# A scheduler that knows VectorE's change of rows, and a newly chosen order of two layers' front pieces

## The chip, the cores and the metric

One core of a Trainium2 chip runs the whole program. The metric is device time in microseconds (us) of one execution, median of the runs.

## The reference

Two encoder layers over 512 tokens of width 1024, float32. In each layer one projection of the normalised input feeds two branches and two gates; the branches are merged, then a feed-forward part (MLP) follows.

```python
h = rms_norm(x, norm1_g[l]) * (1.0 + sc1) + sh1
proj = h @ w_in[l]
y_a = diff_attention(...)            # 4 heads: softmax(q1 k1) - lam * softmax(q2 k2), times v
y_b = gated_deltanet(...)            # 4 heads, both directions, chunks of 64, a triangular solve
merged = g_a * (y_a @ w_branch_a[l]) + g_b * (y_b @ w_branch_b[l])
x = x + gt1 * (merged @ w_out[l])
h = rms_norm(x, norm2_g[l]) * (1.0 + sc2) + sh2
x = x + gt2 * (jnp.square(jax.nn.relu(h @ w_mlp1[l])) @ w_mlp2[l])
```

## The kernel before

The kernel first records all its operations (class `Plan`, `add` at L195) and only then orders them. `schedule` (L250) walks through a model of the engines: each has a time at which it is free, each operation a cost (`cost`, L438) and a delay after what it depends on (`LAG`), and the engine that is free first takes the ready operation with the lowest key. The key is a level (0 for the chains, then evictions, weights, dense products, side work) and, within a level, the place in which the code recorded it. `HOLD` (L424) keeps an engine from starting lower work just before higher work comes in. The resulting order is issued as it stands, so on the chip every engine, and the DMA queue on SyncE (SP), runs its own list strictly in that order and waits on semaphores.

Dense products are split in three: weights are cast to a high part by ScalarE (`whi`), VectorE forms the rest (`wlo`), and TensorE adds three products with the input's parts `hh` and `hl`. So each block of dense weights needs one VectorE subtraction of 128x1024, named `wlo_` and the block, before TensorE can go through it. 24 products of 512 columns make one such block of the gates (`d_g`) or of z (`d_z`); 96 of 256 columns make a pair of blocks of the attention's projections (`d_da`).

The front of a layer is everything up to the branch products. It consists of 28 pieces, recorded in the sequence that `ORDER` (L477) gives for each layer:

- `d`h, `z`h: projections of delta-net head h with their convolutions, and its gate z.
- `a`h (`gdn_a`, L959): norms, the products of keys with keys (`kk`) and the decay, from which the triangular matrices L come; these go through DRAM (`scrL`) into a packed tile `XA`, 32 partitions a head.
- `b0`, `b2` (`gdn_b`, L1032): the triangular inverse of two heads at once, in place in `XA`: a chain of 30 pairs of VectorE operations and a memset, each waiting for the one before. `b0` (heads 0 and 1) works on partitions 0 to 63, `b2` (heads 2 and 3) on 64 to 127.
- `c`h (`gdn_c`, L1047): `XA` goes back through DRAM (`scrT`) into tiles `DT` and `X`; first the products `pn` and `px`, then the state's recurrence over four steps (`pv`, `pS`), the outputs `pog`, and their transposes `ogT`.
- `q`j, `k`j, `v`j: the attention's projections for two heads each; q and k are normalised, rotated, transposed and written to DRAM.
- `t`h (`attention`, L1162): loads q2, k2 and vt of head h, then four blocks of scores `sc`, two maxima and exponentials each, the difference `pr`, transposes `aTp` and products `po`.

```python
for j in range(1, NB - 1):                                   # gdn_b; X is XA's 64 rows of two heads
    dve.tensor_tensor(out=tv, in0=X[:, j+1:NB, j:j+1]..., in1=X[:, j:j+1, 0:j]..., op=ALU.mult)
    op = dve.tensor_tensor(out=X[:, j+1:NB, 0:j], in0=X[:, j+1:NB, 0:j], in1=tv, op=ALU.add)
```

After the pieces come eight blocks of gate products and eight more in turn with the branch products `d_brb` (which need all four `c`), then `d_bra` (which need all four `t`). Gate products, at the dense level, fill TensorE wherever the pieces leave it free. What the code records from the first `d_bra` of a layer to the next front does not depend on the pieces' sequence.

In this text layer one and layer two are l = 0 and l = 1.

Of the kernel before, what the change touches and what calls it, by code (L numbers as in the profile page):

```python
# [23 lines left out]
H = 4  # L24
# [135 lines left out]
class Op:  # L160
    __slots__ = ("eng", "fn", "args", "kw", "key", "preds", "succs", "tiles", "cost", "n", "est", "start", "end",
                 "seq", "ins", "done", "left", "shared", "tried")


class Eng:
    def __init__(self, plan, *names):
# [14 lines left out]
class Plan:  # L181
# [68 lines left out]
    def schedule(self):  # L250
        names = ("pe", "act", "dve", "pool", "sp")
        free_at = {e: 0.0 for e in names}
        ready = {e: [] for e in names}
        future = {e: [] for e in names}
        free = {c: [(0.0, i) for i in range(n)] for c, n in self.slots.items()}
        live = {}
        blocked = {}
        dma_free, flying, shared = 0.0, [], 0.0
        busy, fast = [0.0], [False]
        order = []  # L260
        ops = self.ops
        for op in ops:
            op.left = len(op.preds)
            for q in op.preds.values():
                q.succs.append(op)

        def need(op):
            return [t for t in op.tiles if t.slot is None]

        def offer(op):  # L270

            ts = need(op)
            for t in ts:
                if t.cls not in free:
                    continue
                c, g = free[t.cls], t.grp
                want = sum(u.cls == t.cls for u in ts)
                if len(c) < want + t.keep or live.get(g, 0) >= self.limits.get(g, 1 << 30):
                    return (t.cls, g)
            for t in ts:  # L280
                if t.cls not in free:
                    t.slot = -1
                    continue
                c = free[t.cls]
                best = min(range(len(c)), key=lambda i: c[i])
                t.since, t.slot = c.pop(best)
                live[t.grp] = live.get(t.grp, 0) + 1
            est = max(t.since for t in op.tiles) if op.tiles else 0.0
            for e in op.eng:
                at = max([est] + [q.end + lag(q.eng[0], e) for q in op.preds.values()])  # L290
                heapq.heappush(future[e], (at, op.key, op))
            return None

        def push(op):
            why = offer(op)
            if why:
                heapq.heappush(blocked.setdefault(why, []), (op.key, op))

        def retry(cls):
            for why in [w for w in blocked if w[0] == cls]:  # L300
                while blocked[why]:
                    op = blocked[why][0][1]
                    new = offer(op)
                    if new == why:
                        break
                    heapq.heappop(blocked[why])
                    if new:
                        heapq.heappush(blocked.setdefault(new, []), (op.key, op))

        for op in ops:  # L310
            if not op.left:
                push(op)
        todo = len(ops)
        while todo:
            best = None
            for e in names:
                f, r = future[e], ready[e]
                while f and (f[0][2].done or f[0][0] <= free_at[e]):
                    _, k, op = heapq.heappop(f)
                    if not op.done:  # L320
                        heapq.heappush(r, (k, op))
                while r and r[0][1].done:
                    heapq.heappop(r)
                if r:
                    s = free_at[e]
                elif f:
                    s = f[0][0]
                else:
                    continue
                if best is None or s < best[0]:  # L330
                    best = (s, e)
            if best is None:
                raise RuntimeError("no operation can go on: " + self.held(blocked, order))
            s, e = best
            f, r = future[e], ready[e]
            if not r:
                free_at[e] = s
                while f and f[0][0] <= s:
                    _, k, op = heapq.heappop(f)
                    if not op.done:  # L340
                        heapq.heappush(r, (k, op))
            op = heapq.heappop(r)[1]
            if e != "sp" and op.key[0] >= 0 and HOLD[int(op.key[0])] is not None:

                most, slack = HOLD[int(op.key[0])]
                end = s + op.cost[op.eng.index(e)]
                soon = [x[0] for x in f if x[1][0] < most and x[0] < end - slack and not x[2].done]
                if soon:
                    heapq.heappush(f, (min(soon) + 0.001, op.key, op))
                    continue  # L350

            wait = max([0.0] + [at + lag(o, e) for t in op.tiles if t.cls == "B" for o, at in t.use.items() if o != e])
            if op.shared and e in ("dve", "pool") and shared > s:
                if e == "pool" and wait <= shared:

                    s = wait = shared
                wait = max(wait, shared)
            if wait > s:
                heapq.heappush(f, (wait, op.key, op))
                continue  # L360
            c = op.cost[op.eng.index(e)]
            if e == "pe":

                while s >= (len(busy)) * CLOCK_WINDOW:
                    fast.append(busy[-1] > CLOCK_BUSY * CLOCK_WINDOW)
                    busy.append(0.0)
                busy[-1] += c if op.kw.get("rhs") is None or op.kw["rhs"].shape[-1] > 1 else 0.0
                c *= 1 if fast[-1] else 2
            if any(max(s, free_at[o]) + d < s + c for o, d in zip(op.eng, op.cost) if o != e and o not in op.tried):

                op.tried.add(e)
                continue
            op.done = True
            if op.shared and e in ("dve", "pool"):
                shared = s + c
            op.eng = (e,)
            op.start = s
            if e == "sp":
                dma_free = max(dma_free, op.start + DMA_LEAD) + c
                op.end = dma_free + DMA_TAIL  # L380
                flying.append(op.end)
                free_at[e] = max(op.start + DMA_STEP, flying[-DMA_DEPTH] if len(flying) >= DMA_DEPTH else 0.0)
            else:
                op.end = op.start + c
                free_at[e] = op.end
            order.append(op)
            todo -= 1
            for t in op.tiles:
                t.use[e] = op.end
                t.end = max(t.end, op.end)  # L390
                t.left -= 1
                if not t.left and t.cls in free:
                    free[t.cls].append((t.end + 130.0, t.slot))
                    live[t.grp] -= 1
                    retry(t.cls)
            for q in op.succs:
                q.left -= 1
                if not q.left:
                    push(q)
        return order  # L400
# [21 lines left out]


HOLD = ((0, 600.0),) * 4 + ((3, 100.0),)  # L424
DMA_LEAD, DMA_TAIL, DMA_STEP, DMA_DEPTH = 1100.0, 2400.0, 475.0, 8
CLOCK_WINDOW, CLOCK_BUSY = 3413.0, 0.4
LAG = {"pe": {"pe": 0, "act": 197, "dve": 197, "pool": 197, "sp": 100},
# [10 lines left out]
def cost(eng, fn, dst, ins, kw):  # L438
# [21 lines left out]
    if fn == "memset":  # L460
# [13 lines left out]
GS, NYF, KEEPM = (3, 5), 2, (3, 2)  # L474


ORDER = ("d0 a0 d1 a1 z1 q0 z0 b0 c0 z2 c1 d2 d3 a3 z3 k0 a2 b2 k1 c2 q1 v0 v1 t0 t1 t2 t3 c3",  # L477
         "k1 d0 d1 q0 d2 z1 a0 z0 k0 a1 b0 c0 z2 a2 d3 c1 a3 b2 q1 v0 t0 z3 v1 t1 t2 c2 c3 t3")


@with_exitstack
def encoder(ctx, tc, a, out):
# [3 lines left out]
    pe, act, dve, pool, sp = (Eng(pl, e) for e in ("pe", "act", "dve", "pool", "sp"))  # L486
# [273 lines left out]
    for l in range(DEPTH):  # L760
# [286 lines left out]
        def gdn_c(h, XA):  # L1047
# [24 lines left out]
            for d in range(2):  # L1072
                NTr = Y([P, NT, P], "NT")
                if d == 0:
                    c1, full, ks = slice(0, P - NB), slice(0, P), slice(0, P)
                else:
                    c1, full, ks = slice(NB, P), slice(0, P - NB), slice(0, P - NB)
# [3 lines left out]
                for n in range(1, 4):  # L1081
                    m = P - NB * n
                    rows, cs = (slice(0, m), slice(NB * n, P)) if d == 0 else (slice(0 if n == 1 else P - m, P), slice(0, m))
                    ps, op = four("px", NTr[ks, :, rows], X[ks, d, :, cs], rows, cs)
# [43 lines left out]
            for t in (0, 3, 1, 2):  # L1128
                mms = []
                for d in range(2):  # L1130
                    s = t if d == 0 else NT - 1 - t
# [16 lines left out]
            dve.scalar_tensor_tensor(out=y, in0=pT, scalar=col(O_OUTG + l, 1), in1=ztile[h], op0=ALU.mult, op1=ALU.mult)  # L1148
            yh, yl = Y([P, S], "ybh", F32R), Y([P, S], "ybl", F32R)
            split(yh, yl, y)  # L1150
            ybh.append(yh)
            ybl.append(yl)

        gate = {}

        def opt(*names):
            return [gate[n] for n in names if n in gate]

        ybh, ybl, yah, yal = [], [], [], []


        def attention(h):  # L1162
# [57 lines left out]
            y, yh, yl = Y([P, S], "ya"), Y([P, S], "yah", F32R), Y([P, S], "yal", F32R)  # L1220
            act.activation(y, pT, AF.Copy, scale=subg)
            split(yh, yl, y)
            yah.append(yh)
            yal.append(yl)


        mrg, sga = {}, {}
# [10 lines left out]
        for piece in ORDER[l].split():  # L1238
            kind, h = piece[0], int(piece[1])
# [306 lines left out]
```

## Time and profile before

| | |
|---|---|
| median of 3 runs | 1641.72 us (1641.08 to 1642.95) |
| the profiled execution | 1642.87 us, of which 1641.1 us from first to last instruction |
| TensorE busy | 1597.4 us (97%) |
| VectorE busy | 1349.3 us (82%) |
| ScalarE busy | 834.5 us (51%) |
| GpSimd busy | 162.7 us (10%) |
| mean granted TensorE clock | 0.995 |

The two fronts run from about 45 to 424 us and from 828 to 1234 us of the span; the rest is branch output products and MLP. A busy TensorE is not one at its peak: records of matmuls overlap, so that a stretch can be counted busy although its matmuls start further apart than elsewhere. What a stretch lost is therefore read by counting its matmuls and multiplying by the pace at which they follow each other where nothing is waited for.

### The profile page before, as it was taken

Reading aid. Unit: us, or ns where it says so; the run is one execution under the profiler, and the core shown is the slowest. Engines: PE = TensorE matmul, PEld = TensorE weight load, DVE = VectorE, ACT = ScalarE, POOL = GpSimd, SP = SyncE. Lnnn points to the kernel's source line nnn. Section 1 sums busy time; section 2 is a strip of 40 time slices with the busy share of each in tenths; the row PEclk is TensorE's granted clock in tenths of the full one; section 3 lists DMA queues with packets and bytes.
Section 4 is the critical chain, followed back from the end, with each engine's and each line's share of the span. In section 5 each row is a group of like instructions: output and inputs, shape, how many; then the busy total and the mean of one; then the engine's idle time right before and its main releaser. Section 6 shows DMA issues by size and latency. Waiting matters only on the chain.

```text
span 1641.1 us, 25365 instructions
## 1 busy us (share of the span) xinstructions
PE 1597.4 (97%) x9136; PEld 1379.0 (84%) x9136; DVE 1349.3 (82%) x2995; ACT 834.5 (51%) x1596; POOL 162.7 (10%) x170
## 2 busy tenths in 40 slices
PE   6999999999999999999989999989999999999998
PEld 4788898888899888888888889868888988888887
DVE  7989798799899999985988987998627885767676
ACT  4563352575366645454557435555423674636361
POOL 0232040001300000000023112200003000000000
PEclk9999999999999999999999999999999999999999
DMA  9242625545677585745333331714243625252542
GB/s 378 113 120 67 198 86 169 184 123 184 246 268 272 199 314 178 296 148 211 118 110 104 123 103 65 174 39 123 77 150 121 215 81 197 86 200 83 204 155 78
DMA packets 107728, 260.78 MB, mean 159 GB/s; under 512 B 27841, under 2 KB 40769, under 8 KB 107602
## 3 DMA queue, kind: packets, MB, share of 16 engines
q1 hardware_dynamic: 107602, 259.16, 45.9%
q8 instruction: 72, 1.18, 0.3%
q14 instruction: 54, 0.44, 0.1%
HBM read 242.31 MB, written 16.81 MB: 158 GB/s over the span
## 4 chain that ended last, share of the span: by engine, by line
PE 82%; DVE 12%; DMA 2%; ACT 2%; issue 1%; SPq 1%; POOL 0%; DVEq 0%; ACTq 0%; POOLq 0%
PE d_m L420 18%; PE m2x L420 11%; PE d_g L420 9%; PE d_out L420 6%; PE m2y L420 5%; PE d_da L420 4%; PE d_dn L420 4%; PE d_m1f L420 3%; PE d_brb L420 3%; PE m2z L420 3%; PE d_bra L420 3%; PE px L420 2%; PE d_z L420 2%; PE pv L420 2%; PE pog L420 1%; PE sc L420 1%
## 5 line engine op out<-in xcount | busy, mean ns | idle before, releaser
L420 PE MATMUL d_m<-hh,whi_m 128*128 128x512 f32 x448 | 174.3, 389 | 0.0
L420 PE MATMUL d_m<-hl,whi_m 128*128 128x512 f32 x448 | 174.3, 389 | 0.0
L420 PE MATMUL d_m<-hh,wlo_m 128*128 128x512 f32 x448 | 174.3, 389 | 0.0
L420 DVE TENSOR_TENSOR m2lo<-m,m2hi 128x1024 fp32r<-128x1024 f32 x112 | 132.2, 1217 | 9.1 <-ACT m2hi L420 8.3
L420 ACT CAST m2hi<-m 128x1024 fp32r<-128x1024 f32 x112 | 114.0, 1048 | 48.5 <-DMA m<-in_w_m_dram 23.3
L420 DVE SCALAR_TENSOR_TENSOR ada<-ada,cb 128x1024 f32<-128x1024 f32 x96 | 116.3, 1222 | 3.5 <-DMA ada<-in_ada_w_dram 3.5
L420 PE MATMUL d_da<-whi_da,hl 128*128 128x256 f32 x384 | 110.0, 288 | 0.0
L420 PE MATMUL d_da<-whi_da,hh 128*128 128x256 f32 x384 | 109.5, 287 | 0.0
L420 PE MATMUL d_da<-wlo_da,hh 128*128 128x256 f32 x384 | 108.0, 288 | 0.1
L420 ACT ACTIVATE relu<-d_m 128x512 f32<-128x512 f32 x56 | 33.5, 599 | 145.0 <-PE d_m L420 144.9
L420 PE MATMUL d_g<-hh,whi_g 128*128 128x512 f32 x256 | 102.4, 400 | 0.0
L420 PE MATMUL d_g<-hh,wlo_g 128*128 128x512 f32 x256 | 102.3, 399 | 0.0
L420 PE MATMUL d_g<-hl,whi_g 128*128 128x512 f32 x256 | 101.8, 398 | 0.0
L420 PEld LDWEIGHTS d_m<-hh,wlo_m 128*128 128x128 f32 x448 | 84.1, 188 | 17.5
L420 PEld LDWEIGHTS d_m<-hh,whi_m 128*128 128x128 f32 x448 | 84.1, 188 | 17.5
L420 PEld LDWEIGHTS d_m<-hl,whi_m 128*128 128x128 f32 x448 | 84.1, 188 | 17.3
L420 ACT CAST whi_m<-raw_m 128x1024 fp32r<-128x1024 f32 x56 | 58.8, 1050 | 48.5 <-DMA raw_m<-in_w_mlp_dram 42.6
L420 PE MATMUL d_dn<-hh,wlo_dn 128*128 128x512 f32 (+1 forms) x208 | 79.3, 382 | 0.9 <-DVE wlo_dn L420 0.9
L420 PE MATMUL d_dn<-hl,whi_dn 128*128 128x512 f32 (+1 forms) x208 | 79.2, 381 | 0.0
L420 PE MATMUL d_dn<-hh,whi_dn 128*128 128x512 f32 (+1 forms) x208 | 77.5, 380 | 0.0
L420 DVE TENSOR_TENSOR m<-m,m 128x1024 f32<-128x1024 f32 x64 | 77.5, 1217 | 0.0
L420 DVE TENSOR_TENSOR wlo_m<-raw_m,whi_m 128x1024 fp32r<-128x1024 f32 x56 | 67.9, 1221 | 10.5 <-ACT whi_m L420 10.2
(325 smaller groups left out, 4749.3 us busy)
## 6 DMA issues: line engine op xcount, KB each, us to landing
m<-in_w_m_dram SPq DMA_DIRECT2D x112, 512.0 KB, 4.5
ada<-in_ada_w_dram SPq DMA_DIRECT2D x96, 512.0 KB, 6.1
raw_m<-in_w_mlp_dram SPq DMA_DIRECT2D x56, 512.0 KB, 4.6
raw_g<-in_w_g_dram SPq DMA_DIRECT2D x32, 512.0 KB, 4.5
raw_out<-in_w_out_dram SPq DMA_DIRECT2D x32, 512.0 KB, 4.2
raw_dn<-in_w_dn_dram SPq DMA_DIRECT2D x24, 512.0 KB, 6.0
raw_da<-in_w_da_dram SPq DMA_DIRECT2D x24, 512.0 KB, 4.9
xs<-xT SPq DMA_DIRECT2D x24, 256.0 KB, 2.6
```

The costliest lines, as they stand in the source:

```text
L420: op.ins = getattr(eng[op.eng[0]], fn)(*[real(v) for v in op.args], **{k: real(v) for k, v in op.kw.items()})
```

## The change

In the scheduler's model a VectorE operation whose output lies on other partitions (first and last one compared) than that of the operation before it now starts at least `OTHER_ROWS` = 110 ns after the end of that one. `ORDER` holds a new sequence for both layers. The lists of head outputs (`ybh`, `ybl`, `yah`, `yal`) are filled by head number, since heads no longer come in order. No operation is added or removed but for which engine takes a copy that two engines may take: VectorE gets 11 copies `aT` in place of 6.

```diff
 class Op:
+    def rows(self):
+        return self.kw.get("out", self.args[0] if self.args else None).region()[:2]
...
             c = op.cost[op.eng.index(e)]
+            if e == "dve":
+                rows = op.rows()
+                if rows != dve_rows:
+                    s = max(s, dve_end + OTHER_ROWS)
...
                 free_at[e] = op.end
+                if e == "dve":
+                    dve_rows, dve_end = rows, op.end
...
+OTHER_ROWS = 110.0
...
-ORDER = ("d0 a0 d1 a1 z1 q0 z0 b0 c0 z2 c1 d2 d3 a3 z3 k0 a2 b2 k1 c2 q1 v0 v1 t0 t1 t2 t3 c3",
-         "k1 d0 d1 q0 d2 z1 a0 z0 k0 a1 b0 c0 z2 a2 d3 c1 a3 b2 q1 v0 t0 z3 v1 t1 t2 c2 c3 t3")
+ORDER = ("d0 a0 d1 a1 z1 z0 q0 b0 z2 c0 c1 d3 d2 a3 k0 a2 b2 c2 z3 q1 k1 v1 v0 t0 t2 t3 c3 t1",
+         "d0 k1 d1 q0 d2 z1 a0 z0 d3 k0 z2 a1 b0 c0 a2 v0 t0 c1 a3 b2 q1 c2 z3 v1 c3 t3 t1 t2")
...
-            ybh.append(yh)
-            ybl.append(yl)
+            ybh[h] = yh
+            ybl[h] = yl
...
-        ybh, ybl, yah, yal = [], [], [], []
+        ybh, ybl, yah, yal = ([None] * H for i in range(4))
```

VectorE, layer two, inside `b2` (rows 64x... are its chain, `64x13x18` being 13 rows of 18 elements; 128-row entries belong to the attention heads t0 and t1: maxima `mxv`, sums `cc`, `rc`, the difference `pr`). Before:

```order
2091 L420 TENSOR_TENSOR yal<-ya,yah 128x512
2092 L420 TENSOR_TENSOR XA<-XA,btmp 64x13x18
2093 L420 COPY r_11990<-rc 128x1
2094 L420 TENSOR_TENSOR cc<-sums,rc 128x1
2095 L420 TENSOR_TENSOR btmp<-XA 64x228
2096 L420 TENSOR_TENSOR cc<-cc,nlams 128x1
2097 L420 SCALAR_TENSOR_TENSOR nb<-mxv,qsc 128x1
2098 L420 TENSOR_TENSOR XA<-XA,btmp 64x12x19
2099 L420 SCALAR_TENSOR_TENSOR pr<-pr,cc 128x512
2100 L420 TENSOR_TENSOR btmp<-XA 64x220
```

Now:

```order
2010 L431 TENSOR_TENSOR btmp<-XA 64x168
2011 L431 TENSOR_TENSOR XA<-XA,btmp 64x24x7
2012 L431 TENSOR_TENSOR btmp<-XA 64x184
2013 L431 TENSOR_TENSOR XA<-XA,btmp 64x23x8
2014 L431 TENSOR_TENSOR btmp<-XA 64x198
2015 L431 TENSOR_TENSOR XA<-XA,btmp 64x22x9
2016 L431 TENSOR_TENSOR wlo_g_11987<-raw_g_11849,whi_g_11984 128x1024
2017 L431 TENSOR_TENSOR btmp<-XA 64x210
```

101 instructions of the two attention heads and of others stood between the chain's; six stand there now (one `yal`, five `wlo`), so that VectorE changes between rows that start at 0 and rows that start at 64 22 times in the layer, where it was 126 times (layer one: 18 and 22).

TensorE, layer two, where c2's first products `pn` stand. Before (attention heads t1 and t2 between them):

```order
5150 L420 MATMUL d_g_12509<-hh_8884,whi_g_11996 128x512
5151 L420 MATMUL po<-vt,aT 128x128 x4
5152 L420 MATMUL pn<-DT,L 128x96 x2
5153 L420 MATMUL aTp<-cst,pr 128x128 x4
5154 L420 MATMUL pn<-DT,L 128x96 x2
```

Now (gate blocks alone ahead of them and between them):

```order
5158 L431 MATMUL d_g_12225<-hh_8931,whi_g_12115 128x512
5159 L431 MATMUL d_g_12225<-hl_8940,whi_g_12115 128x512
5160 L431 MATMUL d_g_12225<-hh_8931,wlo_g_12123 128x512
5161 L431 MATMUL pn<-DT,L 128x96
5162 L431 MATMUL d_g_12225<-hh_8937,whi_g_12115 128x512
5163 L431 MATMUL d_g_12225<-hl_8946,whi_g_12115 128x512
5164 L431 MATMUL pn<-DT,L 128x96 x3
```

Between the key products `kk` of a3 and this first `pn`, TensorE's list before held 217 matmuls of 512 columns (`d_g`, `d_z`, `sc`), 138 of 256 (`d_da`), 52 float32 products of 128 columns and 60 transposes; now it holds 236, 33, 26 and 20. The heads t1, t2, t3 stand behind c3 now, where d_brb and the last gate blocks are; t0 stands ahead of a3's `kk`.

The DMA queue, layer two, where t0's loads stand (`vt_...<-vst` writes v of two heads to DRAM). Before:

```order
406 L420 DMA vt_11413<-vst 128x2x256
407 L420 DMA scrL_11425<-LT 32x4x32 x4
408 L420 DMA raw_g_11499<-in_w_g_dram 128x1024
409 L420 DMA raw_g_11519<-in_w_g_dram 128x1024
410 L420 DMA q_11523<-qT_9954 64x2x512 x2
411 L420 DMA k_11536<-kT_9280 64x2x512 x2
412 L420 DMA XA<-scrL_11425 32x1024
413 L420 DMA vt<-vt_11413 128x4x128
```

Now:

```order
397 L431 DMA kT_9757<-qkst 128x2x256
398 L431 DMA vt_10861<-vst 128x2x256 x2
399 L431 DMA raw_g_10876<-in_w_g_dram 128x1024
400 L431 DMA q_10925<-qT_9954 64x2x512 x2
401 L431 DMA k_10944<-kT_9757 64x2x512 x2
402 L431 DMA vt<-vt_10861 128x4x128
403 L431 DMA raw_g_10966<-in_w_g_dram 128x1024
404 L431 DMA gb<-grow_9370 128x512 x2
```

They were issued among a2's transfers and come now right behind c0's first ones, ahead of a2's and a3's `gb`, with 69 `d_da` products and 76 small products of c0 and c1 on TensorE between v0's last product and t0's first `sc`.

## Rows read from the trace of the kernel before

**Rows 1.** Page, part 1 (busy us, share of span, instructions) and part 4

```profile
PE 1597.4 (97%) x9136; PEld 1379.0 (84%) x9136; DVE 1349.3 (82%) x2995; ACT 834.5 (51%) x1596; POOL 162.7 (10%) x170
...
## 4 chain that ended last, share of the span: by engine, by line
PE 82%; DVE 12%; DMA 2%; ACT 2%; issue 1%; SPq 1%; POOL 0%; DVEq 0%; ACTq 0%; POOLq 0%
```

**Rows 2.** Engines' busy time by stretch: b2 of layer one, b2 of layer two

```profile
core 0: us, PE busy (x) PEld busy (x) DVE busy (x) ACT busy (x) POOL busy (x), PEclk, DMA share, GB/s
...
252.14:278.90 26.76, 26.76 (x119) 22.15 (x118) 24.62 (x64) 6.77 (x9) 2.33 (x6) 1.00 0.33 118
...
1051.56:1109.42 57.86, 48.67 (x253) 37.21 (x251) 54.03 (x162) 31.51 (x71) 4.51 (x8) 1.00 0.26 64
```

**Rows 3.** Groups of VectorE instructions in b2 of layer one: count, busy, mean ns

```profile
L420 DVE TENSOR_TENSOR XA<-XA,btmp 64x30 f32<-64x30 f32 (+14 forms) x30 | 9.9, 329 | 1.0
...
L420 DVE TENSOR_TENSOR wlo_g<-raw_g,whi_g 128x1024 fp32r<-128x1024 f32 x4 | 4.9, 1225 | 0.1
```

**Rows 4.** The same in b2 of layer two

```profile
L420 DVE TENSOR_TENSOR XA<-XA,btmp 64x30 f32<-64x30 f32 (+14 forms) x30 | 9.9, 330 | 0.9
```

**Rows 5.** VectorE's timeline (start, duration) in b2 of layer two

```profile
1086.02 0.40 DVE L420 TENSOR_TENSOR XA<-XA,btmp 64x234 f32<-64x234 f32 x1
1086.45 0.15 DVE L420 COPY r<-rc 128x1 f32<-128x1 f32 x1
1086.52 0.15 DVE L420 TENSOR_TENSOR cc<-sums,rc 128x1 f32<-128x1 f32 x1
```

**Rows 6.** VectorE's timeline in b0 of layer one

```profile
120.89 0.33 DVE L420 TENSOR_TENSOR btmp<-XA 64x184 f32<-64x184 f32 x1
121.15 0.73 DVE L420 SCALAR_TENSOR_TENSOR cacc<-d_dn,cols,cacc 128x510 f32<-128x510 f32 x1
121.81 0.33 DVE L420 TENSOR_TENSOR XA<-XA,btmp 64x184 f32<-64x184 f32 x1
```

**Rows 7.** Waits of TensorE in b2 of layer two: total us, times, longest

```profile
PE aTp L420 <- DVE pr L420: 5.3, 6, 1.5
```

**Rows 8.** The chain that ended last, by time: start, us, matmuls following each other

```profile
658.85 43.52 PE d_m L420 x192
...
232.76 15.23 PE d_da L420 x127
...
1006.50 2.01 PE pog L420 x18
```

**Rows 9.** Timelines: last kk products ahead of b2, b2's first instructions, layer two, layer one

```profile
1019.58 1.06 PE L420 MATMUL kk<-kqv 128*128 128x128 f32 x8
...
1051.56 0.20 DVE L420 TENSOR_TENSOR btmp<-XA 64x30 f32<-64x30 f32 x1
...
215.53 0.72 PE L420 MATMUL kk<-kqv 128*128 128x128 f32 x5
...
252.14 0.21 DVE L420 TENSOR_TENSOR btmp<-XA 64x30 f32<-64x30 f32 x1 [2.69 <-DMA XA<-scrL]
252.38 0.21 DVE L420 TENSOR_TENSOR XA<-XA,btmp 64x30 f32<-64x30 f32 x1
```

**Rows 10.** Engines by stretch: from b2's memset to c2's first pn, layer two

```profile
1109.42:1118.60 9.18, 8.65 (x51) 7.31 (x52) 9.08 (x27) 6.36 (x14) 0.10 (x1) 1.00 0.41 106
```

**Rows 11.** Engines by stretch: from c2's first pn to d_bra, layer one and two

```profile
287.39:424.13 136.74, 136.73 (x852) 118.08 (x853) 122.44 (x352) 79.38 (x193) 8.34 (x6) 1.00 0.56 183
...
1118.60:1234.09 115.49, 115.49 (x694) 99.90 (x693) 62.42 (x165) 46.61 (x111) 4.54 (x4) 1.00 0.36 118
```

**Rows 12.** Layer one, b0's memset to c0's first pn: engines, and TensorE's timeline

```profile
162.91:173.52 10.61, 8.02 (x28) 5.90 (x29) 8.68 (x30) 1.89 (x3) 2.94 (x2) 0.84 0.73 209
...
164.21 0.56 PE L420 MATMUL d_z<-hh,wlo_z 128*128 128x512 f32 x1 [3.50 <-DVE wlo_z L420]
```

**Rows 13.** Layer two, t0's loads: DMA queue's timeline, then the chain that ended last

```profile
1028.39 0.38 SPq L420 DMA_DIRECT2D vt<-vst  x1
...
1033.82 7.88 DMA k<-kT
...
1042.90 0.50 PE sc L420
```

More of the change, by code (lines that the diff above doesn't have):

```diff
@@ L259, in schedule @@
         busy, fast = [0.0], [False]
+        dve_rows, dve_end = None, -OTHER_ROWS
         order = []
@@ L1222, in attention @@
             split(yh, yl, y)
-            yah.append(yh)
-            yal.append(yl)
+            yah[h] = yh
+            yal[h] = yl
         mrg, sga = {}, {}
```

## Prediction

> **What bounds the kernel now.** I began with the busy shares and the chain that ended last [rows 1]. TensorE is busy for 97% of the span and makes up 82% of the chain, VectorE 12%. So the kernel is bound by TensorE, except where TensorE waits inside the fronts, and any gain has to be time that TensorE loses there. Its work does not change: the same matmuls are issued in another order.
>
> Then I looked for that loss by stretch [rows 2]. The inverse `b2` is the same chain in both layers, of 30 pairs at equal durations [rows 3, 4]. In layer one it takes 26.76 us, with TensorE busy in all of them. In layer two it takes 57.86 us, with TensorE busy in only 48.67. VectorE is busy there for 54.03 us of the 57.86: this is the one long stretch in which VectorE is the bound. TensorE's own waits agree: it waits mostly for `pr` of the attention heads, 5.3 us in six waits [rows 7].
>
> Why VectorE is full there is seen in its timeline. The chain's instruction of 1086.02 ends at 1086.42, and the next one, on rows from 0 on, starts at 1086.45, 0.03 us after the end. The one after that starts at 1086.52, 0.08 us before its forerunner's end of 1086.60 [rows 5]. In `b0`, on partitions 0 to 63, the sets of rows differ from neighbour to neighbour too, and yet each instruction starts 0.07 us before the end of the one ahead of it: the first ends at 121.22 (120.89 + 0.33) and the next starts at 121.15, that ends at 121.88 and the third starts at 121.81 [rows 6]. So a change of the first row costs some 0.10 us (0.03 plus 0.07), and a change of the last row alone costs nothing. Layer two had 126 changes of the first row, nearly all in `b2`: 126 times 0.104 is 13.1 us of VectorE.
>
> **The change, part by part.** The delay in the scheduler's model costs nothing on the chip; only the order that comes out of it does.
>
> *b2 of layer two.* This is the term that decides. From a3's key products at 1019.58 [rows 9] to c2's first product at 1118.60 [rows 10] the kernel before takes 99.0 us. TensorE's list between them has 217 matmuls of 512 columns, 138 of 256, 52 float32 products (two records each) and 60 transposes. At the paces of undisturbed runs, 43.52/192 = 0.227, 15.23/127 = 0.120 and 2.01/18 = 0.112 us [rows 8], with 0.112 for a transpose too, that is 49.3 + 16.6 + 11.6 + 6.7 = 84.2 us. So 14.8 us are lost.
>
> Now the list has 236, 33, 26 and 20: 53.6 + 4.0 + 5.8 + 2.2 = 65.6 us. Against it stands the chain that c2 needs. From the key products to the start of b2 it takes 32.0 us in layer two and 36.6 in layer one [rows 9]. b2 by itself takes 26.8 us as in layer one, where four `wlo` stood in it [rows 2, 3]; now there are five and a `yal`, at most 1.2 us each less the 0.1 us of waiting that each fills, so about 1.5 us more. From its memset to c2's products are 9.2 us [rows 10]. The sum is 69.5 to 74.1 us, 3.9 to 8.5 us more than TensorE's list fills, and TensorE, which goes through its list in order, waits for so long at `pn`. I take the middle, 6.2. **The term is -14.8 + 6.2 = -8.6 us**, with ends at -10.9 and, if the wait of 8.5 also halves the clock, -4.6: in layer one a wait of 3.50 us was followed by a granted clock of 0.84 over 10.61 us [rows 12], which is 1.2 GHz for about a third of it, 3.4 us, or 1.7 us lost.
>
> What hides the chain is gate and z blocks, 236 matmuls of 512 columns less the eight of `sc`, on TensorE. If their `wlo` came late (they stand between the chain's instructions on VectorE), each block late would cost up to 5.4 us (24 times 0.227).
>
> *The attention heads that leave b2.* t1, t2 and t3 now stand behind c3, with gate blocks and `d_brb` between them. The nearest case is layer one, where four heads stand between c2 and `d_bra`: TensorE is busy in 136.73 us of 136.74, VectorE in 122.44 [rows 11]. In layer two VectorE is busy for 62.42 us of 115.49 in that stretch, so it has 53 us free for what left b2: 54.03 us less the chain's 2 times 9.9 [rows 2, 4], some 34 us, part of which is t0's and goes forward instead. It fits, though not everywhere evenly. I take **+1.5 us**, between 0 and +3.
>
> *t0 beside c0 and c1.* Its loads move past a2's transfers in the DMA queue, and everything behind them there (gate weights, a2's and a3's `gb`) waits if they wait. From the issue of v's last write at 1028.39 to the first `sc` at 1042.90 were 14.5 us, of which the load of k took 7.88 [rows 13]. TensorE now has 69 `d_da` products (8.3 us) and 76 small ones of two records (up to 17.0 us) between v0's products and this `sc`, so the loads should be in. **0 us**, between -1 and +4.
>
> *Layer one.* b2 was alone already and stays so; changes of the first row go from 22 to 18, at 0.1 us each nothing. At b0's end TensorE waited 3.50 us for a `wlo_z` that stood behind the chain, and 10.61 us pass from memset to products [rows 12]. b0's stretch loses 36 VectorE instructions, and TensorE's list ahead of c0 loses 3.9 us of matmuls (4 at 0.227, 14 at 0.120, 12 transposes), so both come earlier by about the same. The wait for `wlo_z` goes; the wait for the DMAs behind the memset is late next. **-1 us**, between -5.2 (the 3.5 and the 1.7 of the clock both gone) and +1.
>
> The lists by head number and the five copies `aT` that VectorE takes from ScalarE (at most 0.7 us each, spread over eight heads) count as nothing: they lie under gate blocks, and are within the second term's range if that cover is gone.
>
> The sum is -8.6 + 1.5 + 0 - 1 = **-8.1 us**. The profiled execution took 1642.87 us, so 1634.8 of its kind; it lies 1.15 us above the median of the runs, 1641.72, which makes **1633.6 us** as a median.
>
> The Trainium skill, "VectorE: DVE Perf Modes", section "Two Vector instructions with no wait between them", speaks against half of the change: there an instruction is held until earlier ones have finished when it starts in another 32-partition quadrant than the last access to that memory, and where it ends does not matter. The trace agrees (0.03 us after the end from row 64 to row 0, 0.07 us before it for rows 0 to 63). By the change's own rule b0 would pay too: in layer two its rows change 113 times where it was 91, 22 times 0.104 or 2.3 us more, and the sum would be -5.8; by the rows it is -8.1.
>
> **The rivals.** *A larger gain.* The chain to b2 is shorter than in either layer, or TensorE's list is behind it anyway, so that the wait at c2 is under 3.9 us, and layer one gives a little more: -14.8 + 1.5 - 2 is -15.3, or 1626.4 us. For it speaks that TensorE is hardly idle ahead of c2's products in layer two even now [rows 10]. Chance 0.13.
>
> *No change.* The loss moves instead of going: the wait at c2 is the long one with the lower clock (-4.6), the three heads behind c3 cost +3, and layer one gives +1, so -0.6: 1641 us. For it speaks that VectorE's total is the same and that it is full in 90% of layer one's tail; against it, that TensorE lost nothing visible in that tail. Chance 0.18.
>
> *Slower.* t0 has the higher rank over c1, and TensorE goes through its list in order: if the loads come more than about 20 us after v0's products, TensorE stands at the first `sc`, and c1, a3 and b2 behind it all start later by as much. The loads wait for `kT` and for v's writes, and the queue is in order. At 10 us late, with the clock's 1.7, the sum is -8.1 + 11.7 = +3.6, or 1645 us; it decides from 8.1 us on. Against it speak the 14.5 us of the rows. Chance 0.12.
>
> *The change does not do what it says.* The model now delays rows 0 to 63 as well, some 110 changes a layer that cost nothing on the chip. The real VectorE then runs ahead of the plan around b0, and waits; the order loses what was arranged for a slower engine, but nothing in the sum above. It belongs to the forecast's own spread.
>
> **How the numbers follow.** A measurement of this kernel can tell about 0.2% (3.3 us) from no change. The forecast (a gain of 4 to 13 us) has 0.57, the larger gain 0.13, no change 0.18, slower 0.12. Faster by over 0.2% takes the first two, 0.70. The range goes from the larger gain, 1626, to the slower case, 1645: it leaves out the worse half of that case and the far end of the larger gain.
>
> **What would show it.** In the changed profile b2 of layer two takes 28 to 30 us with TensorE busy throughout and few VectorE gaps but its own; TensorE waits 4 to 9 us at c2's first `pn`, for `DT`; from there to `d_bra` it is busy throughout; t0's first `sc` does not wait. The forecast is wrong if b2 is as long as before, if TensorE waits over 10 us at `pn` or at t0's `sc`, or if VectorE is full behind c3.

## The result, and the profile after

The changed kernel takes **1633.49 us** (median of 4 runs, 1633.24 to 1633.91), the kernel before 1641.87 beside it (1641.08 to 1642.95): a ratio of 0.9947, 95% interval 0.9934 to 0.9960. Faster, by 8.4 us. The profiled execution spans 1631.5 us.

Parts 1 and 4 of the changed kernel's page, which answer to [rows 1]:

```profile
PE 1593.6 (98%) x9136; PEld 1384.2 (85%) x9136; DVE 1347.1 (83%) x2999; ACT 832.0 (51%) x1592; POOL 167.5 (10%) x170
...
PE 91%; DVE 7%; issue 1%; ACT 1%; DMA 0%; SPq 0%; POOL 0%; DVEq 0%; POOLq 0%; ACTq 0%
```

VectorE's part of the chain that ended last falls from 12% to 7%. Where it went is seen in layer two. The engines' busy time by stretch (columns as in [rows 2]): a3's last `kk` to b2, b2, its memset to c2's first `pn`, from there to `d_bra`:

```profile
1038.88:1065.71 26.83, 26.73 (x169) 23.85 (x168) 25.73 (x106) 17.57 (x52) 10.75 (x15) 1.00 0.30 90
1065.71:1095.95 30.24, 30.24 (x137) 25.07 (x136) 26.71 (x67) 9.37 (x13) 2.51 (x7) 1.00 0.27 97
1095.95:1104.89 8.94, 8.94 (x41) 7.38 (x40) 4.57 (x6) 2.83 (x4) 0.00 (x0) 1.00 0.57 163
1104.89:1224.80 119.91, 119.91 (x754) 103.64 (x753) 82.82 (x252) 65.26 (x158) 5.20 (x5) 1.00 0.41 118
```

b2 takes 30.24 us where it took 57.86 [rows 2], with TensorE busy in all of them; behind it TensorE has no gap at all. Its timeline at c2's first `pn` shows no idle time in brackets, and neither does t0's first `sc`:

```profile
1010.18 0.40 PE L431 MATMUL sc<-kh,qs 128*128 128x512 f32 x1
...
1104.66 0.39 PE L431 MATMUL d_g<-hh,wlo_g 128*128 128x512 f32 x1
1104.89 0.35 PE L431 MATMUL pn<-DT,L 128*128 128x96 f32 x2
```

New losses stand elsewhere. TensorE's waits in the front of layer one (total us, times, longest; the two largest):

```profile
PE tokT L431 <- DVE kqv L431: 7.1, 2, 5.9
PE d_dn L431 <- DVE wlo_dn L431: 2.9, 2, 2.3
```

and its timeline at the longest wait in b0 of each layer:

```profile
129.66 1.09 PE L431 MATMUL tokT<-cst,kqv 128*128 128x128 f32 x4 [5.92 <-DVE kqv L431]
...
980.31 0.45 PE L431 MATMUL d_da<-wlo_da,hh 128*128 128x256 f32 x1 [2.00 <-DVE wlo_da L431]
```

To put all this on one scale I count what TensorE **lost**: the start of a matmul less the sum of the paces of all matmuls ahead of it, with each kind's pace in the kernel before where it waits for nothing, as the prediction did for b2 (by more kinds, so b2 comes out at 15.0 where it said 14.8). In us by stretch, for the two kernels and four of the experiments below (e1: the kernel before with b2 on partitions 0 to 63; e2: the changed kernel without the rule; e4: the rule narrowed to the first row; e5: the kernel before with b0 on partitions 64 to 127):

| stretch | before | changed | e1 | e2 | e4 | e5 |
|---|---|---|---|---|---|---|
| layer one, a1's kk to c0's pn (b0) | 9.8 | 13.7 | 9.5 | 6.6 | 7.2 | 25.2 |
| c0's pn to d_bra | 9.9 | 8.4 | 9.4 | 9.2 | 7.9 | 9.4 |
| d_bra to a1's kk of layer two | 10.3 | 10.7 | 10.4 | 10.4 | 12.2 | 10.4 |
| layer two, a1's kk to c0's pn (b0) | 1.9 | 4.3 | 1.8 | 0.2 | 0.2 | 11.9 |
| c0's pn to a3's kk | 3.5 | 3.0 | 2.8 | 3.7 | 3.6 | 2.8 |
| a3's kk to c2's pn (b2) | 15.0 | 0.4 | 2.3 | 2.3 | 0.6 | 16.0 |
| c2's pn to d_bra | 3.3 | 4.2 | 3.3 | 3.9 | 3.4 | 3.3 |
| sum | 53.7 | 44.7 | 39.5 | 36.3 | 35.1 | 79.0 |

The change wins 14.6 us in b2 of layer two and gives back 3.9 and 2.4 in the two b0.

### The profile page after: what moved, and what is told of

The parts are those of the page before. It is cut to its first block, busy times and chain, and to the rows that moved or that the text cites. A ratio compares the mean times of both kernels' runs of the same rounds, so it can differ in the third digit from the quotient of the medians.

```text
span 1631.5 us, 25364 instructions
## 1 busy us (share of the span) xinstructions
PE 1593.6 (98%) x9136; PEld 1384.2 (85%) x9136; DVE 1347.1 (83%) x2999; ACT 832.0 (51%) x1592; POOL 167.5 (10%) x170
## 4 chain that ended last, share of the span: by engine, by line
PE 91%; DVE 7%; issue 1%; ACT 1%; DMA 0%; SPq 0%; POOL 0%; DVEq 0%; POOLq 0%; ACTq 0%
PE d_m L431 18%; PE d_g L431 11%; PE m2x L431 11%; PE d_dn L431 7%; PE d_da L431 7%; PE d_out L431 6%; PE m2y L431 5%; PE d_m1f L431 3%; PE d_brb L431 3%; PE d_bra L431 3%; PE m2z L431 3%; PE d_z L431 2%; PE px L431 2%; PE sc L431 2%; PE po L431 2%; PE pv L431 2%
## 5 line engine op out<-in xcount | busy, mean ns | idle before, releaser
L431 PEld LDWEIGHTS d_m<-hl,whi_m 128*128 128x128 f32 x448 | 84.1, 188 | 17.3
L431 DVE TENSOR_TENSOR wlo_m<-raw_m,whi_m 128x1024 fp32r<-128x1024 f32 x56 | 68.0, 1222 | 10.4 <-ACT whi_m L431 9.7
```

Of the source, the lines that this page charges most:

```text
L431: op.ins = getattr(eng[op.eng[0]], fn)(*[real(v) for v in op.args], **{k: real(v) for k, v in op.kw.items()})
```

## The experiments

My theory was that the holds at a change of VectorE's first row fill VectorE in b2, and that the new sequence removes them; the rule in the model I took for idle. The rivals: any difference of rows costs (the change's own rule), the heads' work and not the holds fills VectorE, or the rule makes the order.

### e1: b2 on the low rows, nothing else

In the kernel before, four places that name the rows (`gdn_a`, `gdn_b` twice, `gdn_c`); XA is a tile of its own for each two heads:

```diff
-            X = XA[32 * h0:32 * (h0 + n)]
+            X = XA[0:32 * n]
...
-                tv = tmp[32 * h0:32 * (h0 + n), 0:m * j]
+                tv = tmp[0:32 * n, 0:m * j]
...
-        ...XA[32 * h:32 * h + 32]...
+        ...XA[32 * (h & 1):32 * (h & 1) + 32]...
```

> The kernel before with one edit: b2's tile is used on partitions 0 to 63 instead of 64 to 127, in both layers. Every engine's list stays as it was, instruction by instruction. By my theory (an instruction is held about 0.104 us where the first row changes, and only there) layer two's changes of the first row fall from 126 to 8, which is 118 x 0.104 = 12.3 us of VectorE, nearly all in b2: b2 takes 45 to 48 us where it took 57.86, c2's first pn comes 8 to 12 us earlier, and the time is 1630 to 1634 us. By the change's own rule (any other set of rows delays) nothing is saved: the sets differ as often as before, b2 stays at 57 to 58 us and the time within 1.6 us of 1641.9. A third theory, that the heads' own work and not the holds fills VectorE there, gives a gain of at most 3 us.

Measured: **1628.84 us** (before 1641.36), ratio 0.9920, 0.9905 to 0.9934. With the same lists of instructions, b2 of layer two takes 44.21 us:

```profile
1050.57:1094.78 44.21, 44.21 (x250) 37.53 (x249) 43.91 (x165) 29.90 (x69) 4.07 (x8) 1.00 0.32 82
```

and VectorE's timeline shows the same three instructions as [rows 5], with the one behind them:

```profile
1077.05 0.38 DVE L429 TENSOR_TENSOR XA<-XA,btmp 64x234 f32<-64x234 f32 x1
1077.36 0.13 DVE L429 COPY r<-rc 128x1 f32<-128x1 f32 x1
1077.42 0.14 DVE L429 TENSOR_TENSOR cc<-sums,rc 128x1 f32<-128x1 f32 x1
1077.49 0.38 DVE L429 TENSOR_TENSOR btmp<-XA 64x228 f32<-64x228 f32 x1
```

The copy now starts 0.07 us before the end of the XA instruction ahead of it, where it started 0.03 us after. The whole saves 57.86 - 44.21 = 13.65 us over 118 changes, **0.116 us each**. The rule on any rows falls, and so does the rival of the heads' own work: they all still stand in b2, and TensorE loses 2.3 us there instead of 15.0. The time is 1.2 us under the 1630 to 1634 expected: the holds are 0.012 us dearer than read, and nearly all of what VectorE saves reaches TensorE, which loses 12.7 us less in b2.

### e2: the new sequence, the model without the rule

```diff
-                if rows != dve_rows:
-                    s = max(s, dve_end + OTHER_ROWS)
```

> The changed kernel without the rule on rows in the scheduler's model: the new sequence alone. By my theory the sequence makes the gain, and the rule does nothing for layer two: b2 of layer two has six other instructions in it as in the changed kernel, the stretch from layer one's first d_bra to layer two's is within 2 us of the changed kernel's (426.3 to 1224.8, 798.5 us), and the time is 1630.5 to 1636.5 us. The rival is that the rule makes the order what it is: then TensorE waits again behind b2 and the time is 1637 us or more.

Measured: **1624.11 us**, ratio 0.9890, 0.9873 to 0.9906. A miss, by over 6 us and to the better side. The sequence alone gives 17.3 us, and the rule, which I had priced at nothing, takes 9.4 of them back. The table says where: b0 of layer one loses 6.6 us and not 13.7, b0 of layer two 0.2 and not 4.3, while b2 of layer two is a little worse without the rule (2.3 against 0.4).

### e3: the old sequence, the model with the rule

The changed kernel with the two old strings in `ORDER`.

> The kernel before with the rule on rows (110 ns) in the model and its old sequence. The heads t0 and t1 stay in b2 of layer two, with 61 instructions between the chain's where it was 102, and the changes of the first row stay at 128. By my theory most of the loss stays: 1636 to 1643 us. The rival, that the rule is what brings the gain: 1635 us or less.

Measured: **1662.97 us**, ratio 1.0130, 1.0115 to 1.0145: slower by 21.6 us, outside both expectations. b2 still loses 16.9 us, as expected, but the b0 of the two layers lose 12.9 and 8.4, and layer one from c0's `pn` to `d_bra` 19.3. So the rule harms with either sequence, with the old one (21.6 us) more than with the new one (9.4).

### e4: the rule narrowed to the first row

```diff
-                if rows != dve_rows:
+                if dve_rows is None or rows[0] != dve_rows[0]:
```

> The changed kernel with the rule narrowed to the first row: rows 0 to 63 next to rows 0 to 127 are no longer delayed in the model. b0 in layer one then has 86 other instructions between the chain's as in the kernel before (the changed kernel has 50). By my theory the plan is nearer to the chip: layer two as in the changed kernel (within 2 us), and TensorE's 5.9 us wait for kqv in b0 of layer one, which the changed kernel has, becomes shorter; 1629 to 1633.5 us. If the rule on both rows is the right one, b0 is planned too densely and the time is 1636 us or more.

Measured: **1622.66 us**, ratio 0.9885, 0.9870 to 0.9900, against 0.9947 for the changed kernel, and 6.3 us better than the least expected: the rule costs more than the one wait that I had named. What costs is the delay for rows 0 to 63 beside 0 to 127, which the chip does not have. VectorE's timeline where b0 of layer one begins, changed kernel:

```profile
112.40 0.19 DVE L431 TENSOR_TENSOR btmp<-XA 64x30 f32<-64x30 f32 x1
112.52 0.14 DVE L431 TENSOR_TENSOR rqu<-rqu,rqv 128x8 f32<-128x8 f32 x1
112.63 0.21 DVE L431 TENSOR_TENSOR XA<-XA,btmp 64x30 f32<-64x30 f32 x1
112.75 0.14 DVE L431 SCALAR_TENSOR_TENSOR rqr<-rqu,rqr 128x8 f32<-128x8 f32 x1
112.87 0.21 DVE L431 TENSOR_TENSOR btmp<-XA 64x58 f32<-64x58 f32 x1
...
124.11 0.69 DVE L431 SCALAR_TENSOR_TENSOR kqv<-kqv,cacc 128x512 f32<-128x512 f32 x1 [2.96 <-ACT kqv L431]
...
128.84 0.68 DVE L431 SCALAR_TENSOR_TENSOR kqv<-kqv,cacc 128x512 f32<-128x512 f32 x1
```

and with the narrowed rule:

```profile
113.19 0.19 DVE L431 TENSOR_TENSOR btmp<-XA 64x30 f32<-64x30 f32 x1
113.31 0.14 DVE L431 TENSOR_TENSOR rqu<-rqu,rqv 128x8 f32<-128x8 f32 x1
113.38 0.15 DVE L431 SCALAR_TENSOR_TENSOR rqu<-rqr 128x8 f32<-128x8 f32 x1
113.46 0.19 DVE L431 TENSOR_TENSOR XA<-XA,btmp 64x30 f32<-64x30 f32 x1
...
119.97 0.67 DVE L431 SCALAR_TENSOR_TENSOR kqv<-kqv,cacc 128x512 f32<-128x512 f32 x1
...
125.41 0.67 DVE L431 SCALAR_TENSOR_TENSOR kqv<-kqv,cacc 128x512 f32<-128x512 f32 x1
```

With the full rule one other instruction stands between two of the chain, with the narrowed one at first two. So the chain runs ahead of the other work there, and `kqv`, for which TensorE's `tokT` waits, comes 3.4 to 4.1 us later, though b0 starts 0.8 us earlier.

VectorE's order is not all of it: the lists of the other engines were planned around it too. The 2.96 us that VectorE waits are for ScalarE, whose list in the changed kernel has the next block's `cacc`, which waits for TensorE, ahead of this `kqv`:

```profile
122.87 0.69 ACT L431 ACTIVATE cacc<-d_dn,cols 128x512 f32<-128x512 f32 x1 [3.75 <-PE d_dn L431]
123.46 0.62 ACT L431 ACTIVATE kqv<-cacc 128x512 f32<-128x512 f32 x1
```

and with the narrowed rule behind it:

```profile
118.86 0.62 ACT L431 ACTIVATE kqv<-cacc 128x512 f32<-128x512 f32 x1
...
123.65 0.69 ACT L431 ACTIVATE cacc<-d_dn,cols 128x512 f32<-128x512 f32 x1 [3.23 <-PE d_dn L431]
```

And TensorE's list reaches the `tokT` of 129.66 us after 51 products `d_dn`, where 60 stand ahead of it with the narrowed rule, about 2 us of cover less. No run separates the three. Busy times from 112.40 to 146.00 us, changed kernel:

```profile
112.40:146.00 33.60, 25.35 (x106) 20.70 (x105) 29.59 (x78) 11.33 (x29) 2.39 (x6) 0.85 0.24 86
```

and with the narrowed rule:

```profile
112.40:146.00 33.60, 33.58 (x194) 29.23 (x193) 33.60 (x82) 15.69 (x35) 2.28 (x6) 1.00 0.27 93
```

In the changed kernel VectorE itself is idle for 4 us while TensorE, idle for 8, waits for it; b0 as a whole is no shorter (50.80 us, and 50.66 with the narrowed rule).

### e5: b0 on the high rows

The opposite of e1, in the kernel before: all four heads on partitions 64 to 127.

```diff
-            X = XA[32 * h0:32 * (h0 + n)]
+            X = XA[64:64 + 32 * n]
```

(and the other three places in the same way)

> The kernel before with the opposite edit: b0's tile on partitions 64 to 127 instead of 0 to 63 (b2 stays on 64 to 127). Every engine's list stays as it was. Changes of the first row go from 22 to 142 in layer one and from 126 to 212 in layer two. By my theory each costs about 0.104 us of VectorE: 120 x 0.104 = 12.5 us in b0 of layer one, where TensorE already waits for VectorE, and 86 x 0.104 = 8.9 us in b0 of layer two, where about half is hidden. c0's first pn of layer one comes 8 to 12 us later, and the time is 1650 to 1660 us. By the change's own rule (any other set of rows) the sets differ as often as before and the time stays within 1.6 us of 1641.5.

Measured: **1665.92 us**, ratio 1.0147, 1.0132 to 1.0163: slower by 24.2 us. b0 of layer one and of layer two, e5:

```profile
112.31:176.82 64.51, 51.03 (x309) 44.83 (x307) 60.73 (x146) 21.44 (x43) 9.85 (x12) 0.95 0.17 57
938.60:993.41 54.81, 47.66 (x273) 41.79 (x273) 51.48 (x119) 17.91 (x31) 7.58 (x10) 0.94 0.23 82
```

and in the kernel before:

```profile
112.18:162.91 50.73, 47.60 (x309) 42.70 (x308) 50.70 (x148) 21.45 (x43) 9.57 (x12) 1.00 0.21 73
924.73:969.64 44.91, 44.38 (x268) 39.01 (x267) 44.07 (x121) 17.37 (x31) 7.18 (x10) 1.00 0.28 97
```

64.51 - 50.73 = 13.78 us over 120 changes, and 54.81 - 44.91 = 9.90 over 86: **0.115 us each**, twice, as in e1. The direction was right and the time too small, since I let half of layer two's be hidden. Nothing was: TensorE lost 15.4 and 10.0 us more, with the granted clock at 0.95 and 0.94.

### e6: the changed kernel with b2 on the low rows

The edit of e1.

> The changed kernel, rule and sequence as they are, with b2's tile on partitions 0 to 63. The order stays the same in every engine's list; changes of the first row go from 22 to 8 in layer two and from 18 to 8 in layer one. By my theory the holds are all that the place of the rows is worth, so there is next to nothing left: 14 x 0.104 = 1.5 us at most, and 1631.5 to 1634 us. If the low rows gain in another way (transfers, transposes), they gain here as in the kernel before: about 1621 us.

Measured: **1633.14 us**, ratio 0.9950, 0.9934 to 0.9967; the changed kernel's is 0.9947. Low rows by themselves gain nothing; e1's gain was the holds.

### e7 and e8: sequences and rows together

e7 is e2 with the edit of e1; e8 has the new sequence in layer one only.

> The new sequence without the rule in the model, and b2's tile on partitions 0 to 63: changes of the first row go from 25 to 11 in layer two. By my theory up to 1.5 us less than the new sequence alone (1624.1): 1621 to 1624.5 us. If what is left behind b2 there (2.3 us lost up to c2's pn) comes from VectorE's holds, it goes; if from TensorE's list, it stays.

> Layer one with the new sequence, layer two with the old one, no rule in the model, and b2's tile on partitions 0 to 63. The two layers' orders are independent of each other, so by the stretches of the earlier runs layer one gives 3.5 to 4.5 us and layer two 13 to 14 us against the kernel before: 1623 to 1626 us. That would say that in layer two the rows are worth what the new sequence is worth. If the sequence of layer two has a gain of its own besides the holds, 1628 us or more.

Measured: **1623.13 us** (0.9884, 0.9870 to 0.9899) and **1623.08 us** (0.9886, 0.9872 to 0.9901). In e8 the old sequence, with t0 and t1 in b2, loses only 1.1 us from a3's `kk` to c2's `pn`. So in layer two the whole gain of the new sequence over the old one is had by the four places that name rows.

### e9 and e10: the rule on both rows at 30 and at 55 ns

```diff
-OTHER_ROWS = 110.0
+OTHER_ROWS = 30.0
```

(and 55.0)

> The changed kernel with the rule on both rows kept, but at 30 ns instead of 110. With 30 ns the scheduler still puts 86 other instructions into b0's chain of layer one, as without the rule; with 110 ns it puts 50. My theory is that the rule costs through this step alone: the plan spaces b0's chain so widely that VectorE's other work comes late. Then this kernel behaves as the new sequence without the rule, 1621 to 1627 us, and TensorE is busy throughout from 112 to 146 us. A rival, that the cost grows in proportion to the delay (9.4 us at 110 ns), gives 1626.7 us with some of the wait for kqv left.

> The same at 55 ns, where the scheduler puts only 46 other instructions into b0's chain of layer one. By the theory of the step it behaves as the changed kernel: between kk and c0's first pn of layer one TensorE loses 11 to 15 us (the new sequence without the rule: 6.6), it waits about 6 us for kqv, and the time is 1630 to 1637 us. In proportion to the delay it would be 1628.8 us.

Measured: **1626.78 us** (0.9908, 0.9890 to 0.9925) and **1637.52 us** (0.9975, 0.9965 to 0.9986). The same stretch as above, 30 ns:

```profile
112.40:146.00 33.60, 33.38 (x190) 28.80 (x189) 33.27 (x82) 15.68 (x35) 2.28 (x6) 1.00 0.27 87
```

and 55 ns:

```profile
112.40:146.00 33.60, 27.54 (x125) 22.61 (x124) 32.53 (x77) 12.43 (x29) 2.40 (x6) 0.90 0.25 83
```

The 30 ns run is what both the theory (1621 to 1627) and proportion (1626.7) gave, and its interval overlaps that of e2; 55 ns decides. Proportion falls there: 55 ns costs more than 110, and the time is just over the 1630 to 1637 expected. That b0's stretch starves where the plan steps from 86 to some 50 instructions is borne out at 30, 55 and 110 ns, but the place of the loss is not: at 55 ns the stretch up to c0's `pn` lost 10.1 us, not 11 to 15, the wait for `kqv` was 3.4 us, not 6, and 16.4 us were lost behind it up to `d_bra` (9.2 in e2), 4.1 of them in one wait of `oT` for `oa`. That a delay the chip does not have makes the plan worse is shown at 55 and 110 ns; by how much, and where it comes out, depends on the whole order.

### e11: the old sequence with the narrowed rule

> The kernel before, its sequence kept, with the rule narrowed to the first row (110 ns). Layer one's b0 keeps its 86 instructions. In layer two b2 has 61 others instead of 102, but the changes of the first row stay at 128. By my theory a model that knows the holds cannot remove them while the heads stand beside b2: layer one as before (d_bra at 424 us, give or take 2), layer two still loses 8 to 16 us between a3's kk and c2's first pn, 1634 to 1643 us. If knowing the holds is enough: below 1632 us.

Measured: **1641.09 us**, ratio 0.9997, 0.9987 to 1.0007: no change. a3's `kk` to c2's `pn` loses 14.0 us. With this sequence a model that knows the holds doesn't avoid them; where the pieces stand, or on which rows, does.

### e12: all three together

The new sequence, the narrowed rule, b2 on the low rows.

> A version meant to beat both: the new sequence, the rule narrowed to the first row, and b2's tile on partitions 0 to 63, so that almost no change of the first row is left (8 and 10). By my theory the three overlap in what they save: 1621 to 1624 us, no better than the measured 1622.7 and 1623.1 of the pairs by more than 1.5 us. If their gains add up: 1619 us or less.

Measured: **1624.04 us**, ratio 0.9885, 0.9868 to 0.9903. Like e2, e4, e7 and e8, between 1622.7 and 1624.1 and not to be told apart. All of them beat both kernels. Their gains overlap, since each removes the same holds of layer two, by the sequence or by the rows.

## Why the prediction was right, and where it was not

The total (1633.6 forecast, 1633.49 measured) came out because errors of opposite sign met, which is luck: b2 gave 6.0 us more than forecast, and layer one and b0 of layer two took 5.6 us more.

**b2 of layer two, -8.6 forecast, -14.6 measured.** The mechanism is as told: TensorE waited for a VectorE that the holds filled. The mis-sized part is the wait of 6.2 us at c2's `pn`, which did not come. The chain of 69.5 to 74.1 us was at most 26.83 + 30.24 + 8.94 = 66.0 us, against 65.6 of matmuls. b2 (28.3 forecast) and the way from the memset (9.2) were close; the step that failed is "from the key products to the start of b2 it takes 32.0 us in layer two and 36.6 in layer one": it took 26.83. Both of those stretches had other pieces beside the chain, and I took their length for the chain's own; that these pieces made it so long is the likely reason, but no run tests it. The rival of a larger gain had named just this.

**The delay in the model, 0 forecast, +9.4 measured (e2).** This is the larger failure. "The delay in the scheduler's model costs nothing on the chip; only the order that comes out of it does" is true, but I priced that order only where the sequence moves pieces, and wrote off b0 with "nothing in the sum above". The listing of VectorE in b0 of layer one would have shown one instruction where two had stood; the prediction even had their count, 36 fewer, and read it as time saved. These 9.4 us are no further term: 6.7 of them stand in layer one's, and b0 of layer two has 4.1, less the 1.9 that b2 loses more without the rule. The alternative that I worked out, the chip obeying the change's rule for 2.3 us, was rightly put aside: e1 and e5 show that only the first row counts. The Trainium skill, "VectorE: DVE Perf Modes", section "Two Vector instructions with no wait between them", says the same of the start quadrant. The runs agree, and put 0.115 to 0.116 us on each change.

**Layer one, -1 forecast, +2.2 measured** (13.7 - 9.8 in b0, 8.4 - 9.9 behind it, less the 0.2 that the changed kernel is ahead at a1's kk). The wait for `wlo_z` did fall, from 3.5 us to 0.2; what came late was not the DMA behind the memset but `kqv`, some 34 us earlier. Without the rule the term is -4.5 (e2), inside the range given.

**t0 beside c0 and c1, 0 forecast.** Right as to its loads: `sc` does not wait, and c0's `pn` to a3's `kk` loses 3.0 us for 3.5. But 2.4 us came in ahead of c0, in a b0 of layer two that the sum did not hold: the 2.00 us wait for `wlo_da`, and a granted clock of 0.81 from there to c0's `pn`. Without the rule this b0 loses 0.2 us (e2), so the loss is the rule's and not t0's.

**The heads behind c3, +1.5 forecast, +0.9 measured**, with VectorE busy in 82.82 us of 119.91, far from full.

For the sum of the measured terms: 2.2 + 0.4 + 2.4 - 0.5 - 14.6 + 0.9 = -9.2 us between the profiled executions, whose spans differ by 9.6.

## What to carry to other kernels

Look first at which partitions interleaved VectorE instructions start on: moving a small chain to the row where its neighbours start costs nothing, and gave 12.5 us by itself, where the best version here gave 18.7. A scheduler's model needs the chip's rule and not one that merely contains it: a delay that the chip shows only where the first row changes, applied to every change of rows, cost 9.4 us. And where a change alters a model, price the order that comes out in the stretches it does not mention, above all where one engine is already the bound.

## What the runs showed of the hardware

The price of a change of first row comes out alike in three stretches with different neighbours, 0.116, 0.115 and 0.115 us, against 0.104 read from single gaps. (Those are the changes of a whole layer; inside the stretches alone stand 120, 118 and 84, which makes 0.114, 0.117 and 0.118.) Part of the difference to 0.104 is in the records: the `XA` instruction and the copy behind it take 0.40 and 0.15 us in [rows 5], and 0.38 and 0.13 in e1. And where VectorE is the bound TensorE can lose more than the holds themselves, 25.4 us for 23.7 in e5, where its granted clock is 0.95 and 0.94; that the clock makes the whole difference is not shown. In the changed kernel after the wait of 5.92 us:

```profile
129.66:137.46 7.80, 5.47 (x18) 4.57 (x19) 7.80 (x14) 2.17 (x6) 1.20 (x3) 0.50 0.00 0
```

The granted clock is 0.50 there, the lower level of 1.2 GHz: four `tokT` take 1.09 us, where they take 0.60 at 2.4 GHz in the same stretch of e4:

```profile
126.40 0.60 PE L431 MATMUL tokT<-cst,kqv 128*128 128x128 f32 x4
```
